# Second-half lower weights by a ScalarE negation and an accumulating transfer in the even layer

## Chip, cores and metric

One core of one Trainium2 chip runs the kernel. The metric is the device time of one execution in microseconds (us); lower is better.

## What is computed

Two layers of a post-norm encoder trunk on 256 tokens of width 2048, in fp32. Both layers are `x = LN(alpha*x + mixer(x))`, then `x = LN(alpha*x + relu(x @ w1)**2 @ w2)`. Only the mixer of the first ("even") layer is touched:

```python
h = x @ w_in
u = h[..., :S5_WIDTH]
q, k, v, gate = jnp.split(h[..., S5_WIDTH:], 4, axis=-1)
...
y = jax.nn.gelu((y_fwd + y_bwd + d_skip.astype(F32) * uf).reshape(bsz, L, S5_WIDTH))
s5_out = (y * jax.nn.sigmoid(y @ w_glu.astype(F32) + b_glu.astype(F32))).astype(x.dtype)
...
ret_out = (o.reshape(bsz, L, RET_WIDTH) * jax.nn.silu(gate.astype(F32))).astype(x.dtype)
return jnp.concatenate([s5_out, ret_out], axis=-1) @ w_out
```

`y_fwd` and `y_bwd` are diagonal state-space scans over the sequence in both directions ("S5"), `o` is retention, a decayed linear attention.

## The kernel before

All weights (356 chunks of 1 MB) pass once through the core in chunks of 512 x 512 numbers, in the order that `weight_order` lists. In this text chunk *n* is the *n*-th of that list, counted from 0: chunks 0 to 39 are `even_w_in`, 40 to 47 `even_w_out`, 48 to 51 `w_glu`, 52 to 59 `even_w_out` again, and then come the two MLPs and the odd layer.

Matmuls run in fp32r, a rounded fp32, so each fp32 number is taken as an upper half (the number rounded to fp32r) plus a lower half (the number minus its upper half), and a product is three matmuls: upper x upper, upper x lower, lower x upper (`mm3`, L186 to L188). `wload` prepares a chunk: a transfer on SP's queue writes it into the tile `wraw` (L169), and then for each of the two halves *b* of the chunk (two of its four 128-row slices each) ScalarE copies it into `whi`, rounding (L178), and VectorE writes `wlo = wraw - whi` (L179).

There are two `wraw` buffers. The transfer of chunk *n* therefore waits until the last reader of chunk *n - 2* is done. In the even layer `whi` and `wlo` have four buffers each, which is two chunks, so half *b* of chunk *n* also waits until TensorE is through with half *b* of chunk *n - 2*. `weights` fetches one chunk ahead. TensorE wants the second half of a chunk in the middle of that chunk's matmuls.

Beside the weights, VectorE and ScalarE work on the S5 mixer and on retention. This work is hung on a table of ticks (one tick is one chunk, each with three phases: `pre`, `mid`, `post`): `s5_plan` starts at tick 7. `s5_in` builds `Fm` on VectorE, turns it on TensorE (L635), multiplies (L645) and turns again (L654); `s5_scan` is a chain of small VectorE operations on `G`; `s5_out` builds `Em` on VectorE, copies `bb` and `G` into `stg` on ScalarE (L696 to L701) and multiplies (L712, L716). Its part `kern` sends a small table `kc` to DRAM (`kd`, L733), `load_m` reads it back in eight transfers (`Mt`, L739), and `load_y` fetches the result (`yg`, L768). `kd`, `Mt`, `yg` and the four `u_dr` stores (L983) are issued by GpSimd (POOL); everything else by SP. `run_phase` places the work of a tick after the two instructions `self.after` that `wload` returned for the chunk. The framework then settles the order on each engine; an engine takes its instructions in that order, and a waiting instruction holds all behind it.

Of the kernel before, what the change touches and what calls it, by code (L numbers as in the profile page):

```python
# [10 lines left out]
F32 = mybir.dt.float32  # L11
# [3 lines left out]
ALU = mybir.AluOpType  # L15
# [36 lines left out]
class Trunk:  # L52
# [54 lines left out]
    def weight_order(self):  # L107
# [6 lines left out]
        for l in r2:  # L114
            if l == 1:
                o += [("odd_w_in", n, kc) for n in (4, 5, 0, 1, 2, 3) for kc in r4]
                o += [("odd_w_out", *x) for x in self.ODD_OUT] + [("odd_w_out", 3, kc) for kc in r4]
            for g in range(NG + 1):
# [22 lines left out]
    AS, AT, AO = 0, 6, 8  # L141

    W1, W2 = 6, 3
    ODD_OUT = [(0, 0), (0, 1), (0, 2), (1, 0), (1, 1), (1, 2), (0, 3), (1, 3), (2, 0), (2, 1), (2, 2), (2, 3)]

    def weights(self, name, *idx):
# [15 lines left out]
    def wload(self, src):  # L162

        nc = self.nc
        raw = self.wp.tile([128, 4, 512], F32, name="wraw", tag="wraw")

        first = self.wnext == 1
        for part in ((slice(0, 2), slice(2, 4)) if first else (slice(0, 4),)):
            self.last = nc.sync.dma_start(raw[:, part], src[:, part]).ins  # L169
        res = []  # L170
        for b in range(2):
            pool = self.wpools[self.wcount % len(self.wpools)]
            self.wcount += 1
            hi = pool.tile([128, 2, 512], F32R, name="whi", tag="whi")
            lo = pool.tile([128, 2, 512], F32R, name="wlo", tag="wlo")
            r = raw[:, 2 * b:2 * b + 2, :]
            for k in ((slice(0, 1), slice(1, 2)) if first else (slice(0, 2),)):
                c = nc.scalar.copy(hi[:, k], r[:, k]).ins  # L178
                d = nc.vector.tensor_tensor(lo[:, k], r[:, k], hi[:, k].bitcast(F32), op=ALU.subtract).ins  # L179
            res += [(hi[:, 0, :], lo[:, 0, :]), (hi[:, 1, :], lo[:, 1, :])]  # L180
        return res, (c, d)

# [996 lines left out]
    def odd_out(self, mix, hp):  # L1179
# [11 lines left out]
        if hp is None:  # L1191
            self.gemm_n(lhs, self.ODD_OUT, 4, src, evac)
            return
# [126 lines left out]
```

## Time and profile before

| what | value |
|---|---|
| median of 3 runs | 2149.88 us (2149.59 to 2151.16) |
| profiled execution: its own time | 2148.78 us |
| profiled execution: span of the trace | 2147.0 us |
| TensorE (PE) busy | 2117.7 us, 99% |
| VectorE (DVE) busy | 1449.6 us, 68% |
| ScalarE (ACT) busy | 1010.9 us, 47% |
| GpSimd (POOL) busy | 57.2 us, 3% |
| mean granted TensorE clock | 0.997 |

The even layer's mixer fills about the first 440 us of the span. Shares over the whole span hide what holds in that part, so it has to be read by stretches. A busy TensorE row includes time in which matmuls overlap in the pipeline: the step from one matmul of 512 columns to the next is about 0.23 us, while the row of one lasts about 0.39 us.

### The profile page before, as it was taken

Reading aid. Unit: us, or ns where it says so; the run is one execution under the profiler, and the core shown is the slowest. Engines: PE = TensorE matmul, PEld = TensorE weight load, DVE = VectorE, ACT = ScalarE, POOL = GpSimd, SP = SyncE. Lnnn points to the kernel's source line nnn. Section 1 sums busy time; section 2 is a strip of 40 time slices with the busy share of each in tenths; the row PEclk is TensorE's granted clock in tenths of the full one; section 3 lists DMA queues with packets and bytes.
Section 4 is the critical chain, followed back from the end, with each engine's and each line's share of the span. In section 5 each row is a group of like instructions: output and inputs, shape, how many; then the busy total and the mean of one; then the engine's idle time right before and its main releaser. Section 6 shows DMA issues by size and latency. Waiting matters only on the chain.

```text
span 2147.0 us, 28354 instructions
## 1 busy us (share of the span) xinstructions
PE 2117.7 (99%) x11218; PEld 1768.9 (82%) x11218; DVE 1449.6 (68%) x2098; ACT 1010.9 (47%) x1387; POOL 57.2 (3%) x102
## 2 busy tenths in 40 slices
PE   9998999999999999999999999999999999999998
PEld 8786777878888888888888888888888888888886
DVE  8999986787655656656566777667555655656556
ACT  4554465564443444434445556465443444434441
POOL 0000232000000000000000000000000000000000
PEclk9999999999999999999999999999999999999999
DMA  8534567565555555555555644555555555555562
GB/s 266 178 119 137 155 193 224 194 227 206 195 188 187 194 189 187 192 194 182 194 196 197 207 150 139 171 193 205 196 185 189 195 188 187 194 191 183 195 231 102
DMA packets 82550, 402.35 MB, mean 187 GB/s; under 512 B 30833, under 2 KB 31089, under 8 KB 35569
## 3 DMA queue, kind: packets, MB, share of 16 engines
q1 hardware_dynamic: 79280, 393.26, 53.9%
q0 software_dynamic: 3136, 7.28, 1.4%
q8 instruction: 88, 1.44, 0.3%
q14 instruction: 46, 0.37, 0.1%
HBM read 395.33 MB, written 5.18 MB: 187 GB/s over the span
## 4 chain that ended last, share of the span: by engine, by line
PE 91%; DVE 7%; issue 0%; DMA 0%; ACT 0%; POOL 0%; SPq 0%; DVEq 0%; POOLq 0%
PE ps L281 22%; PE ps L186 18%; PE ps L188 18%; PE ps L187 18%; PE ps L282 11%; DVE wlo L179 2%; DVE G L64 1%; DVE xt L64 1%; DVE sc L64 1%; PE ps L716 1%; PE ps L635 1%; PE ps L349 0%; DVE Fm L64 0%; DVE Em L64 0%; DMA x<-in_x_dram 0%
## 5 line engine op out<-in xcount | busy, mean ns | idle before, releaser
L179 DVE TENSOR_TENSOR wlo<-wraw,whi 128x1024 fp32r<-128x1024 f32 (+1 forms) x714 | 867.3, 1220 | 619.9 <-ACT whi L178 619.2
L178 ACT CAST whi<-wraw 128x1024 fp32r<-128x1024 f32 (+1 forms) x714 | 746.3, 1050 | 982.7 <-PE ps L188 567.0
L281 PE MATMUL ps<-xt,whi 128*128 128x512 f32 x2048 | 722.3, 397 | 0.0
L282 PE MATMUL ps<-xt,wlo 128*128 128x256 f32 x2048 | 575.0, 281 | 0.0
L281 PEld LDWEIGHTS ps<-xt,whi 128*128 128x128 f32 x2048 | 384.9, 188 | 93.1
L186 PE MATMUL ps<-whi,hh 128*128 128x512 f32 (+1 forms) x1032 | 400.4, 388 | 0.0
L188 PE MATMUL ps<-whi,hl 128*128 128x512 f32 (+1 forms) x1032 | 400.1, 388 | 0.0
L187 PE MATMUL ps<-wlo,hh 128*128 128x512 f32 (+1 forms) x1032 | 399.9, 387 | 0.0
L282 PEld LDWEIGHTS ps<-xt,wlo 128*128 128x128 f32 x2048 | 387.3, 189 | 0.5
L188 PEld LDWEIGHTS ps<-whi,hl 128*128 128x128 f32 x1032 | 193.8, 188 | 40.2
L186 PEld LDWEIGHTS ps<-whi,hh 128*128 128x128 f32 x1032 | 193.8, 188 | 39.8
L187 PEld LDWEIGHTS ps<-wlo,hh 128*128 128x128 f32 x1032 | 193.8, 188 | 39.0
L186 PE MATMUL ps<-whi,xt 128*128 128x512 f32 x512 | 207.1, 405 | 0.2 <-ACT whi L178 0.2
L187 PE MATMUL ps<-wlo,xt 128*128 128x512 f32 x512 | 200.7, 392 | 1.3 <-DVE wlo L179 1.3
L188 PE MATMUL ps<-whi,xt 128*128 128x512 f32 x512 | 201.5, 394 | 0.0
L188 PEld LDWEIGHTS ps<-whi,xt 128*128 128x128 f32 x512 | 96.1, 188 | 21.8 <-issue 1.3
L187 PEld LDWEIGHTS ps<-wlo,xt 128*128 128x128 f32 x512 | 96.4, 188 | 20.5 <-DVE wlo L179 1.7
L186 PEld LDWEIGHTS ps<-whi,xt 128*128 128x128 f32 x512 | 96.1, 188 | 19.9 <-issue 1.8
L64 DVE TENSOR_TENSOR acc<-ps,acc 128x512 f32<-128x512 f32 (+1 forms) x113 | 72.4, 678 | 16.9 <-PE ps L188 16.9
L102 ACT COPY s<-ps 128x256 f32<-128x256 f32 x120 | 42.8, 374 | 25.1 <-PE ps L282 24.9
L92 POOL TENSOR_TENSOR rstd<-rs_ve,mhalf 128x1 f32<-128x1 f32 x8 | 6.9, 857 | 1765.3 <-DVE rs_ve L77 1765.3
L186 PE MATMUL ps<-whi,om 128*128 128x512 f32 x128 | 50.5, 395 | 0.0
(212 smaller groups left out, 1679.7 us busy)
## 6 DMA issues: line engine op xcount, KB each, us to landing
wraw<-in_mlp_w_dram SPq DMA_DIRECT2D x256, 1024.0 KB, 4.9
wraw<-in_even_w_in_dram SPq DMA_DIRECT2D x39, 1024.0 KB, 5.0
wraw<-in_odd_w_in_dram SPq DMA_DIRECT2D x24, 1024.0 KB, 4.9
wraw<-in_even_w_out_dram SPq DMA_DIRECT2D x16, 1024.0 KB, 5.0
wraw<-in_odd_w_out_dram SPq DMA_DIRECT2D x16, 1024.0 KB, 4.8
Mt<-kd POOLq DMA_DIRECT2D x64, 64.0 KB, 3.9
wraw<-in_w_glu_dram SPq DMA_DIRECT2D x4, 1024.0 KB, 4.8
lng<-in_ln_g_dram SPq DMA_DIRECT2D x4, 1024.0 KB, 6.9
```

The lines of the kernel that those rows point to most:

```text
L64: self.nc.vector.tensor_tensor(o, a, b, op=op)
L92: self.nc.gpsimd.tensor_tensor(out, ve, self.mhalf[:, 0:w], op=ALU.pow)
L102: self.nc.scalar.copy(lo[:, i], ps[i][:, 1])
L178: c = nc.scalar.copy(hi[:, k], r[:, k]).ins
L179: d = nc.vector.tensor_tensor(lo[:, k], r[:, k], hi[:, k].bitcast(F32), op=ALU.subtract).ins
L186: nc.tensor.matmul(o, lhsT=ah, rhs=bh, start=first, stop=False)
L187: nc.tensor.matmul(o, lhsT=ah, rhs=bl, start=False, stop=False)
L188: nc.tensor.matmul(o, lhsT=al, rhs=bh, start=False, stop=last)
L281: nc.tensor.matmul(o, lhsT=wh[:, c], rhs=x, start=(k == 0), stop=False)
L282: nc.tensor.matmul(o[:, 0], lhsT=wl[:, c], rhs=x[:, 0], start=False, stop=(k == 4 * nk - 1))
L635: nc.tensor.transpose(ps[:, i * 128:(i + 1) * 128], st["F"][:, r, i, :], self.ident)
L716: nc.tensor.matmul(y[64 * (i % 2):64 * (i % 2) + 64, i // 2 * 128:i // 2 * 128 + 128], lhsT=S[:, r, i, 32:96], rhs=E[:, r, i, :], start=Fa ...
```

## The change

For chunks 6 to 48 (`wnext` counts from 1, so `DMA_LO` is 43 chunks), the second half no longer gets its lower half from VectorE. ScalarE writes `whi` as before, and also writes minus the raw weights, rounded to fp32r, into `wlo`; a transfer issued by GpSimd then adds the raw weights onto `wlo` in place. The first half of these chunks, and all other chunks, are as before. `wload` returns as second member of `self.after` the last VectorE subtraction, which in these chunks is that of the first half.

```diff
+    DMA_LO = range(7, 50)
...
             r = raw[:, 2 * b:2 * b + 2, :]
-            for k in ((slice(0, 1), slice(1, 2)) if first else (slice(0, 2),)):
-                c = nc.scalar.copy(hi[:, k], r[:, k]).ins
-                d = nc.vector.tensor_tensor(lo[:, k], r[:, k], hi[:, k].bitcast(F32), op=ALU.subtract).ins
+            if b == 1 and self.wnext in self.DMA_LO:
+
+                c = nc.scalar.copy(hi, r).ins
+                nc.scalar.mul(lo, r, -1.0)
+                nc.gpsimd.dma_start(lo.bitcast(F32), r, accum_op=ALU.add)
+            else:
+                for k in ((slice(0, 1), slice(1, 2)) if first else (slice(0, 2),)):
+                    c = nc.scalar.copy(hi[:, k], r[:, k]).ins
+                    d = nc.vector.tensor_tensor(lo[:, k], r[:, k], hi[:, k].bitcast(F32), op=ALU.subtract).ins
```

In the changed kernel all lines from here on stand 2 to 8 further down: L178 is L181 or L186, L179 is L187, L186 to L188 are L194 to L196; L182 is the negation and L183 the transfer.

ScalarE, one chunk in the middle of `s5_in` (chunks 22 and 23). Before:

```order
L178 CAST whi<-wraw 128x1024
L649 COPY Vs<-ps 128x256
L636 COPY FT<-ps 128x512 x2
L178 CAST whi<-wraw 128x1024
L658 COPY G<-ps 128x2x128
L178 CAST whi<-wraw 128x1024
```

In the changed kernel:

```order
L181 CAST whi<-wraw 128x1024
L657 COPY Vs<-ps 128x256
L644 COPY FT<-ps 128x512 x2
L186 CAST whi<-wraw 128x1024
L666 COPY G<-ps 128x2x128
L182 ACTIVATE wlo<-wraw 128x1024
L181 CAST whi<-wraw 128x1024
```

The negation is one more ScalarE instruction per chunk; here it stands ahead of the copy of the second half, as in 15 of the 43 chunks; in the other 28 (6 to 14, 25, 30, 31 and 33 to 48) it stands behind it.

GpSimd, two of the eight S5 output groups (`kd`, `Mt`, `yg`). Before:

```order
L733 DMA kd<-kc 128x240
L768 DMA yg<-yd 128x256
L739 DMA Mt<-kd 16x8x128 x8
L733 DMA kd<-kc 128x240
L768 DMA yg<-yd 128x256
L739 DMA Mt<-kd 16x8x128 x8
```

In the changed kernel:

```order
L741 DMA kd<-kc 128x240
L776 DMA yg<-yd 128x256
L183 DMA wlo<-wraw 128x1024
L747 DMA Mt<-kd 16x8x128 x8
L183 DMA wlo<-wraw 128x1024
L741 DMA kd<-kc 128x240
L776 DMA yg<-yd 128x256
L183 DMA wlo<-wraw 128x1024
L747 DMA Mt<-kd 16x8x128 x8
L183 DMA wlo<-wraw 128x1024
```

Every second accumulating transfer of this stretch stands behind the eight `Mt` issues, which wait for `kd` to land.

TensorE, the second half of chunk 8. In the changed kernel:

```order
L194 MATMUL ps<-whi,xt 128x512
L195 MATMUL ps<-wlo,xt 128x512
L196 MATMUL ps<-whi,xt 128x512
L194 MATMUL ps<-whi,xt 128x512 x2
L195 MATMUL ps<-wlo,xt 128x512
L196 MATMUL ps<-whi,xt 128x512
L195 MATMUL ps<-wlo,xt 128x512
```

A matmul with the upper half has been put ahead of the first one with the lower half of that chunk's second part (the row with x2). In the even layer of the kernel before, such a pair stands at two places, the first halves of chunks 8 and 10; in the changed kernel it stands at 16, most of them in second halves of chunks 33 to 46.

## Rows read from the trace of the kernel before

**Rows 1.** The page, parts 1 and 2: whole span, then 40 slices.

```profile
PE 2117.7 (99%) x11218; PEld 1768.9 (82%) x11218; DVE 1449.6 (68%) x2098; ACT 1010.9 (47%) x1387; POOL 57.2 (3%) x102
...
DVE  8999986787655656656566777667555655656556
```

**Rows 2.** Busy time by stretch (us; then PE clock, DMA share, GB/s).

```profile
60.00:200.00 140.00, 135.01 (x903) 106.58 (x904) 134.64 (x276) 75.65 (x127) 2.18 (x3) 1.00 0.44 145
200.00:300.00 100.00, 94.53 (x726) 70.13 (x724) 96.15 (x225) 53.48 (x101) 25.18 (x47) 0.98 0.56 161
300.00:350.00 50.00, 49.75 (x360) 37.68 (x356) 34.61 (x64) 26.73 (x45) 18.64 (x35) 1.00 0.80 235
350.00:440.00 90.00, 90.00 (x437) 74.55 (x438) 64.32 (x78) 45.86 (x59) 1.14 (x2) 1.00 0.56 193
500.00:1150.00 650.00, 650.00 (x3268) 550.98 (x3267) 381.37 (x418) 280.41 (x321) 0.00 (x0) 1.00 0.56 191
```

**Rows 3.** Waits of PE, 60 to 440 us: total us, times, longest.

```profile
PE ps L716 <- ACT stg L699: 2.8, 1, 2.8
PE ps L712 <- DVE Em L64: 2.7, 2, 2.1
PE ps L712 <- DVE Em L82: 2.0, 2, 1.0
PE ps L187 <- DVE wlo L179: 1.3, 1, 1.3
```

**Rows 4.** Timeline of ScalarE at the scan's end.

```profile
195.60 0.82 ACT L699 COPY stg<-G 64x248 f32<-64x248 f32 x2 [8.25 <-DVE G L64]
```

**Rows 5.** Busy time by stretch: the one at the lower clock.

```profile
208.40:211.80 3.40, 3.36 (x28) 2.65 (x29) 3.40 (x8) 1.29 (x5) 0.00 (x0) 0.52 0.00 0
```

**Rows 6.** Groups of instructions by line and form, 60 to 440 us.

```profile
L179 DVE TENSOR_TENSOR wlo<-wraw,whi 128x1024 fp32r<-128x1024 f32 x105 | 127.1, 1220 | 31.5 <-ACT whi L178 31.0
L178 ACT CAST whi<-wraw 128x1024 fp32r<-128x1024 f32 x105 | 109.1, 1051 | 119.8 <-PE ps L188 83.0 <-DMA wraw<-in_even_w_out_dram 16.0 <-PE ps L281 5.2
```

**Rows 7.** DMA issues: count, KB each, median us to landing.

```profile
u_dr<-u POOLq DMA_DIRECT2D x4, 256.0 KB, 2.9
...
wraw<-in_mlp_w_dram SPq DMA_DIRECT2D x256, 1024.0 KB, 4.9
...
xr<-in_x_dram SPq DMA_DIRECT2D x2, 1024.0 KB, 9.3
```

**Rows 8.** The tile wraw, 69.6 to 80 us: chunks 10, 11 and 12.

```profile
DMA to landing us min/median/max: 4.8/5.7/7.6
```

**Rows 9.** Timelines of SP, ACT and PE: chunks 8 and 10.

```profile
69.70 0.43 SPq L169 DMA_DIRECT2D wraw<-in_even_w_in_dram  x1
70.23 0.38 SPq L169 DMA_DIRECT2D wraw<-in_even_w_in_dram  x1
...
59.84 2.00 ACT L178 CAST whi<-wraw 128x1024 fp32r<-128x1024 f32 x2
75.44 2.00 ACT L178 CAST whi<-wraw 128x1024 fp32r<-128x1024 f32 x2 [1.67 <-DMA wraw<-in_even_w_in_dram]
...
65.62 0.39 PE L187 MATMUL ps<-wlo,xt 128*128 128x512 f32 x1
80.80 0.39 PE L187 MATMUL ps<-wlo,xt 128*128 128x512 f32 x1
```

**Rows 10.** Timelines of PE and DVE: first uses in chunks 42, 45, 46.

```profile
340.25 1.23 DVE L179 TENSOR_TENSOR wlo<-wraw,whi 128x1024 fp32r<-128x1024 f32 x1 [1.48 <-ACT whi L178]
351.39 0.39 PE L187 MATMUL ps<-wlo,rr 128*128 128x512 f32 x1
366.48 0.39 PE L187 MATMUL ps<-wlo,rr 128*128 128x512 f32 x1
371.92 0.39 PE L187 MATMUL ps<-wlo,rr 128*128 128x512 f32 x1
```

**Rows 11.** Timelines of POOL and PE: an S5 output group; chunks 12 and 41.

```profile
61.24 0.72 POOL L983 DMA_DIRECT2D u_dr<-u  x1 [20.89 <-DVE u L64]
218.82 0.61 POOL L733 DMA_DIRECT2D kd<-kc  x1 [13.17 <-DVE G L64]
223.17 4.20 POOL L739 DMA_DIRECT2D Mt<-kd  x8 [3.74 <-DMA kd<-kc]
...
93.17 0.39 PE L187 MATMUL ps<-wlo,xt 128*128 128x512 f32 x1
340.93 0.40 PE L187 MATMUL ps<-wlo,rr 128*128 128x512 f32 x1
```

## Prediction

> **What bounds the kernel now.** Read the page first: over the span TensorE is busy 99%, VectorE 68% [rows 1]. By that, relief for VectorE is worth nothing. The line of 40 slices below it says otherwise for the start: VectorE is near full in the first seven slices. So the second view is the busy time by stretch [rows 2]: from 60 to 300 us VectorE is busy 134.6 + 96.2 of 240 us, in the MLP 381 of 650. In the same 240 us TensorE is busy 229.5, and in the MLP all of its time. TensorE sets the end; what can be won is the time for which it waits in the even layer, no more.
>
> Third, its waits there [rows 3]. Four entries of 2.8, 2.7, 2.0 and 1.3 us make 8.8. Three name VectorE. The largest names ScalarE's copy into `stg`, but that copy itself stood 8.25 us for VectorE's scan on `G` [rows 4], so it is VectorE too. After these waits TensorE ran for 3.4 us at a clock of 0.52, its lower level [rows 5]; at the full clock that work takes half, so 1.7 us more is lost. **At most 10.5 us can be won**, 0.5% of the run.
>
> **What the change takes away.** 43 subtractions of 1.22 us [rows 6] leave VectorE, 52 us in all. 27 of them (chunks 8 to 34) lie between 60 and 300 us: 33 us off a stretch in which it is busy for 231 of 240. Its backlog should dissolve, and I count all four waits and the clock as won: **-10.5 us**.
>
> **What it adds.** ScalarE gets 43 negations. No row shows this form; I price it like the copy of the same size, 1.05 us [rows 6], together 45 us. ScalarE has room (53 of 100 us busy at the worst [rows 2]). GpSimd gets 43 issues; the store of 256 KB occupied it for 0.72 us [rows 11], so about 31 us on an engine that is idle for 97%: nothing by themselves. The wait that matters is another: `wlo` of the second half is done when a transfer has landed, and `wraw` is free for the load after the next only then too.
>
> **The price of one accumulating transfer** (512 KB read, 512 KB read and added to, 512 KB written) stands in no row. Below, a plain transfer: between 256 KB in 2.9 us and 1 MB in 4.9 us [rows 7], a third of the way, gives 3.6 us. That counts only the bytes that are moved. If both things it reads count, it is like a load of 1 MB, 4.9 us alone. It is seldom alone, since the DMA engines are busy for half of the time [rows 2]; where two loads were issued 0.5 us apart the median was 5.7 and the longest 7.6 us [rows 8, 9]. Nothing excludes a slower addition; the slowest median of a 1 MB transfer is 9.3 us [rows 7], which I take as the upper end. I take 5.7 us, the nearest row for 1 MB of reading beside another transfer, and 5.7 us for the load beside it.
>
> Here a rule stands against the trace. The rows for 256 KB and 1 MB give 3.6 us for 512 KB. The Trainium skill ("DMA: Bandwidth & Descriptors", section on the anatomy of one DMA) fits a GpSimd transfer as 2.0 us plus the bytes at 436 GB/s; that is an estimate of 3.2 us for 512 KB, and by it the sum would be that of the first rival below. [...]
>
> **Three places where this costs.** The two `wraw` buffers form a ring. One turn takes a load 5.7, two copies 2.0 [rows 9], the negation 1.05, the transfer 5.7: 14.45 us, and must take no longer than two chunks on TensorE.
>
> *Start of the ring.* Chunk 8: the copies end at 59.84 + 2.00 = 61.84 [rows 9], negation to 62.9, landing at 68.6. TensorE took that half at 65.62, after the 1.3 us wait that I count as won, so would want it at 64.3: it waits 4.3. Chunk 10: the load is issued at 69.70, held there by the `U` transfers ahead of it on SP's queue and not by the ring; copies end at 77.4, landing at 84.2; wanted at 80.80 - 1.3 + 4.3 = 83.8: 0.4. Together **+4.7 us**.
>
> *End of the ring.* From chunk 43 the S5 work is over and TensorE takes a chunk in 5.44 us [rows 10], two in 10.88. The ring is 3.57 short per two chunks, so 10.7 us over chunks 43 to 48. There is a lead: in chunk 42 `wlo` was ready at 341.48 and wanted at 351.39 [rows 10], 9.9 us; the new path is longer by 1.05 + 5.7 - 1.23 = 5.5, leaving 4.4. So 10.7 - 4.4 = **+6.3 us**. These are chunks in which VectorE has 26 of 90 us free [rows 2]: there the change relieves nobody.
>
> *Between.* From chunk 12 to 41 a chunk takes (340.93 - 93.17)/29 = 8.54 us [rows 11], two 17.1: the ring fits. But on GpSimd's queue every second transfer from chunk 26 on stands behind `Mt`: this waits until `kd` has landed (4.35 us from issue to issue) and issues for 4.20 us [rows 11]. A transfer that meets it lengthens its turn to 18.65. That is 1.55 over, for one turn in two, and the lead of some 10 us swallows most; where chunks are shorter than the mean it does not. DMA engines are also 80% busy from 300 to 350 [rows 2]. I put **+2 us**, from 0 to 8. SP's queue: the loads now wait for a landing, and `c` and `yd` behind them with it; at 5.7 us the landing comes about when VectorE's late subtraction did in this stretch (the scan held ScalarE and VectorE for 8 us [rows 4]), so nothing.
>
> **Sum:** -10.5 + 4.7 + 6.3 + 2 = **+2.5 us** on the profiled 2148.78, that is 2151.3; the median lies 1.1 higher: **2152.4 us**. A measurement of this kernel can tell about 0.2%, or 4.3 us, from no change.
>
> **Rivals.**
>
> *A cheap transfer (faster).* At 3.6 us with loads at 4.9 the ring turns in 11.55. Chunk 8 lands at 66.5, a wait of 2.2; chunk 10 at 82.1, 0.4. In chunks 43 to 48 the ring is short by 0.34 per chunk, 2.0, under the lead of 6.5: nothing. Between, 15.75 with `Mt` fits too. Sum -10.5 + 2.6 = -7.9: **2142 us**. For it: the small transfers land in 2.9 us. Against: three streams, not two. Chance 0.33.
>
> *A dear transfer (slower): the ring becomes the bound.* The point is 17.1 us per turn, a transfer of 8.3 us with loads at 5.7; up to there it costs at the three places alone. At 7.6 us [rows 8] the turn is 16.35: chunk 8 and 10 give 6.2 + 0.4, the end (16.35 - 10.88)/2 x 6 = 16.4 less a lead of 2.5 is 13.9, between 5 (turns behind `Mt` 3.4 over, half of 16 chunks, less the lead). Sum -10.5 + 6.6 + 13.9 + 5 = +15: **2165 us**. At 9.3 us the turn is 18.05: 0.5 us for each of 29 chunks comes on top, 14, with 8 at the start, 20 at the end and 10 between, **2191 us**. Against it: no transfer of this size took that long in most stretches. For it: an addition in the transfer is unknown, and the order on TensorE has 16 places, not 2, where an upper half is put ahead of a late lower half. Chance 0.18.
>
> *ScalarE becomes late.* The first copy of a chunk now stands at the head of ScalarE until a later load lands, with `G`, `Vs` and `stg` behind it. If that keeps half of the waits, the gain is 5.2, not 10.5: +7.7, **2157.6 us**. For it: TensorE's largest wait already ended on a ScalarE copy. Against: ScalarE is half idle. Chance 0.09.
>
> **How the numbers follow.** My forecast gets 0.40, by itself 2146 to 2158 (transfer between 4.9 and 6.3 us). Faster by over 0.2% is nearly all of the cheap transfer and 0.05 of the forecast: 0.37. Within 0.2%: 0.26 of the forecast and little of the rest, 0.27. Slower: 0.09 of the forecast, the dear transfer, late ScalarE: 0.36. The range goes from a transfer at 2.9 us (chunk 8 lands 0.7 earlier, and 1 us for rows that disagree: 2140) to one at about 8.3 us: 2175. It leaves out the upper half of the dear case and little below.
>
> **What would show it.** In the changed trace: the median from issue to landing of `wlo<-wraw` (5.7 by the forecast, under 4.3 or over 6.5 by the rivals); TensorE's waits on `stg` and `Em` gone; new waits of TensorE for `wlo` at chunks 8, 10 and 45 to 48 and hardly elsewhere; VectorE at 80 to 85% from 60 to 300 us; the low clock gone. If waits for `wlo` are spread over all chunks, the ring binds and I am wrong; if there are none, I overpaid for the transfer; if `stg` and `Em` still hold TensorE, the relief of VectorE was not what they waited for.

## Result and profile after

| what | before | changed |
|---|---|---|
| median of 4 runs | 2150.52 us | 2207.01 us (2204.76 to 2212.54) |
| span of the profiled execution | 2147.0 us | 2204.4 us |
| ratio of the medians, 95% interval | | 1.0265 [1.0252, 1.0277] |

The changed kernel is 56.5 us slower. The forecast was 2152.4 us, and the range ended at 2175.

Busy time by stretch of the changed kernel, in the columns of [rows 2] (PE, PEld, DVE, ACT, POOL, then the PE clock, the DMA share, GB/s):

```profile
60.00:200.00 140.00, 124.20 (x779) 96.71 (x779) 104.80 (x226) 78.92 (x123) 15.06 (x18) 0.96 0.74 190
200.00:300.00 100.00, 91.76 (x690) 69.54 (x689) 86.55 (x223) 56.48 (x107) 30.35 (x50) 0.97 0.82 205
300.00:350.00 50.00, 46.68 (x367) 34.16 (x365) 27.72 (x49) 30.71 (x57) 17.54 (x30) 0.97 0.91 210
350.00:440.00 90.00, 72.40 (x374) 54.72 (x371) 30.90 (x51) 37.06 (x45) 20.29 (x32) 0.96 0.83 219
```

VectorE did get its relief: 104.80 us busy where it was 134.64. TensorE lost more. Two columns say where to look: the DMA engines, busy for 0.44 to 0.80 of the time before, are now busy for 0.74 to 0.91, and the granted clock is at 0.96 to 0.97 in all four stretches. That costs up to 13.7 us, where in [rows 2] it costs up to 2.

TensorE's waits of 60 to 440 us in the changed kernel, to be held against [rows 3] (all the waits of before in this stretch make 10.3 us, these 47.5):

```profile
PE ps L761 <- DVE y L64: 15.8, 5, 6.4
PE ps L195 <- DMA wlo<-wraw: 12.3, 6, 3.6
PE ps L662 <- ACT Vs L657: 5.2, 3, 3.3
PE ps L290 <- DMA wlo<-wraw: 4.3, 2, 4.1
PE ps L643 <- DVE Fm L64: 3.4, 3, 3.0
PE ps L194 <- ACT whi L186: 2.3, 3, 1.2
PE ps L720 <- DVE Em L64: 1.3, 1, 1.3
```

The waits of [rows 3] have shrunk as forecast: `stg` is gone, and `Em` has fallen from 4.7 to 1.7 us (with 0.4 us on L82). In their place stand 16.6 us for the transferred `wlo`, and 15.8 us for `y`, a tile of the S5 output part that no line of the change touches.

DMA issues of 60 to 440 us (count, KB each, median us from issue to landing). Before, the same view had 5.0 for `wraw<-in_even_w_in_dram`, 3.9 for `Mt`, 2.8 for `yd`, 3.8 for `yg`:

```profile
wraw<-in_even_w_in_dram SPq DMA_DIRECT2D x31, 1024.0 KB, 5.9
wlo<-wraw POOLq DMA_DIRECT2D x41, 512.0 KB, 5.8
...
Mt<-kd POOLq DMA_DIRECT2D x64, 64.0 KB, 6.2
...
yd<-yv SPq DMA_DIRECT2D x64, 16.0 KB, 5.0
yg<-yd POOLq DMA_DIRECT2D x8, 128.0 KB, 5.0
```

The new transfer lands in 5.8 us in the median, almost the 5.7 of the forecast. But single ones took from 4.5 to 11.3 us, and 12 of the 43 took more than 7.6. The loads and small transfers of these lines have all become slower beside it.

One turn of a `wraw` buffer in the changed kernel, chunk 12 to chunk 14 (timelines of SP, ACT, POOL, SP: start, us, instruction; the number in brackets is the idle time before it):

```profile
92.71 0.33 SPq L171 DMA_DIRECT2D wraw<-in_even_w_in_dram  x1
99.85 1.05 ACT L186 CAST whi<-wraw 128x1024 fp32r<-128x1024 f32 x1 [2.38 <-DMA wraw<-in_even_w_in_dram]
100.81 1.05 ACT L181 CAST whi<-wraw 128x1024 fp32r<-128x1024 f32 x1
101.76 1.05 ACT L182 ACTIVATE wlo<-wraw 128x1024 fp32r<-128x1024 f32 x1
103.10 0.84 POOL L183 DMA_DIRECT2D wlo<-wraw  x1 [10.45 <-ACT G L666]
107.75 0.33 SPq L171 DMA_DIRECT2D wraw<-in_even_w_in_dram  x1
```

The turn takes 15.04 us: 7.14 until the copy starts, 2.96 for copies and negation, 0.29 of handing over, 4.65 from issue to the next load. The next turn of this buffer takes 16.4 (to 124.19). Of the 43 loads that need a buffer back from a transfer (chunks 8 to 50), 34 are issued within 0.2 us of its landing, and SP waits for these landings 35 times, 249.9 us in all:

```profile
SPq L171 <- DMA wlo<-wraw: 249.9, 35, 11.8
```

SP stood for about as long before: 97.9 us for VectorE's subtraction, and 252.5 us with the entries that name VectorE's other instructions. So the waiting itself is not the loss; the later end of it is. The median turn of a buffer, from load to load, grew from 15.0 to 16.0 us for chunks 10 to 24, and from 17.7 to 20.0 us for chunks 25 to 42.

Nine loads come later still than the landing that frees their buffer. Five of these (chunks 34, 36, 38, 40 and 42, by 1.0 to 6.5 us) stand behind the eight `yd` issues of an S5 output group on SP's queue. Such a group of issues takes 3.6 to 4.7 us before, and 4.5 to 14.9 us in the changed kernel. The longest is the one behind the two `xr` transfers (timelines of SP: before; then in the changed kernel, with SP's wait for `xr`):

```profile
331.21 4.72 SPq L763 DMA_DIRECT2D yd<-yv  x8
```

```profile
355.68 14.93 SPq L771 DMA_DIRECT2D yd<-yv  x8
371.64 3.75 SPq L171 DMA_DIRECT2D wraw<-in_even_w_out_dram  x2
SPq L771 <- DMA xr<-in_x_dram: 10.4, 2, 5.7
```

The first of the two loads at 371.64 is that of chunk 42. Its buffer was free at 365.11, when the transfer of chunk 40 had landed.

How a late load reaches the S5 part is seen at 384 to 397 us (timelines of ACT, DVE, PE of the changed kernel):

```profile
394.47 1.04 ACT L186 CAST whi<-wraw 128x1024 fp32r<-128x1024 f32 x1 [9.76 <-DMA wraw<-in_even_w_out_dram]
395.55 1.22 DVE L187 TENSOR_TENSOR wlo<-wraw,whi 128x1024 fp32r<-128x1024 f32 x1 [5.06 <-ACT whi L186]
396.69 0.42 DVE L64 TENSOR_TENSOR y<-ps,y 128x256 f32<-128x256 f32 x1
397.16 0.69 PE L761 MATMUL ps<-ident,y 128*128 128x128 f32 x2 [5.03 <-DVE y L64]
```

ScalarE's copy of the first half of chunk 44 waits for a load that was issued late: at 387.29, on the landing of chunk 42's transfer, whose own load had stood behind `yd`. VectorE's subtraction waits for the copy. `y` stands behind the subtraction in VectorE's order, and TensorE stands for `y`, which had nothing to do with weights. The wait of 3.3 us for `y` at 337 us has the same chain, behind the load of chunk 38. In the longest one, 6.4 us at 279 us, `y` stands behind VectorE's scan on `G`; why the scan is late there was not followed further.

Last, a thing at the LayerNorm behind the even layer. VectorE's timeline before, and then in the changed kernel:

```profile
443.67 0.15 DVE L77 TENSOR_SCALAR rs_ve<-mv 128x1 f32<-128x1 f32 x1
444.52 1.46 DVE L79 TENSOR_SCALAR acc<-acc,mv,rstd 128x512 f32<-128x512 f32 x3 [0.69 <-POOL rstd L92]
```

```profile
495.81 0.14 DVE L77 TENSOR_SCALAR rs_ve<-mv 128x1 f32<-128x1 f32 x1
497.17 2.36 DVE L187 TENSOR_TENSOR wlo<-wraw,whi 128x1024 fp32r<-128x1024 f32 x2 [1.22 <-ACT whi L186]
499.45 1.91 DVE L79 TENSOR_SCALAR acc<-acc,mv,rstd 128x512 f32<-128x512 f32 x4
```

In the changed kernel two subtractions have come ahead of the normalisation, and one of them waits for its copy. TensorE waits 5.7 us for `acc` there, before 1.4:

```profile
PE ps L357 <- DVE acc L79: 5.7, 1, 5.7
```

The last accumulating transfer had landed at 436.24, so this comes from the order on VectorE and not from a transfer under way. The granted clock fell in that wait too, to 0.50 from 498.95 to 505.78 us.

Where the time was lost can be read from the first use of `wlo` in each chunk; how much later it comes than before is called the delay here: +0.1 us at chunk 7, +5.3 at 8, +10.2 at 9, +22.9 at 24, then +15.1 at 26 (VectorE's waits of 195 to 212 us, won back), +28.8 at 41, +50.1 at 49, +50.6 at 58, +57.6 at 60 behind the LayerNorm.

### The profile page after: what moved, and what is told of

Same layout as the page of the kernel before. It is cut to its first block, busy times and chain, and to the rows that moved or that the text cites. A ratio compares the mean times of both kernels' runs of the same rounds, so it can differ in the third digit from the quotient of the medians.

```text
span 2204.4 us, 28496 instructions
## 1 busy us (share of the span) xinstructions
PE 2132.1 (97%) x11218; PEld 1775.0 (81%) x11218; DVE 1408.1 (64%) x2055; ACT 1042.7 (47%) x1428; POOL 96.1 (4%) x145
## 3 DMA queue, kind: packets, MB, share of 16 engines
q1 hardware_dynamic: 79280, 393.26, 52.9%
## 4 chain that ended last, share of the span: by engine, by line
PE 85%; DMA 8%; DVE 3%; issue 1%; ACT 1%; SPq 1%; POOL 0%; DVEq 0%; ACTq 0%; POOLq 0%
PE ps L289 22%; PE ps L194 16%; PE ps L195 16%; PE ps L196 16%; PE ps L290 11%; DMA wlo<-wraw 3%; DMA wraw<-in_even_w_in_dram 2%; DMA wraw<-in_even_w_out_dram 1%; DVE wlo L187 1%; PE ps L357 1%; DMA wraw<-in_w_glu_dram 1%; DMA yd<-yv 1%; DVE G L64 0%; ACT whi L186 0%; DMA x<-in_x_dram 0%
## 5 line engine op out<-in xcount | busy, mean ns | idle before, releaser
L187 DVE TENSOR_TENSOR wlo<-wraw,whi 128x1024 fp32r<-128x1024 f32 (+1 forms) x671 | 815.2, 1220 | 659.4 <-ACT whi L186 659.1
L186 ACT CAST whi<-wraw 128x1024 fp32r<-128x1024 f32 (+1 forms) x671 | 701.3, 1050 | 974.5 <-PE ps L196 493.9
L194 PE MATMUL ps<-whi,hh 128*128 128x512 f32 (+1 forms) x1032 | 400.5, 388 | 0.0
L196 PE MATMUL ps<-whi,hl 128*128 128x512 f32 (+1 forms) x1032 | 400.1, 388 | 0.0
L196 PEld LDWEIGHTS ps<-whi,hl 128*128 128x128 f32 x1032 | 193.8, 188 | 40.1
L194 PEld LDWEIGHTS ps<-whi,hh 128*128 128x128 f32 x1032 | 193.8, 188 | 39.6
L194 PE MATMUL ps<-whi,xt 128*128 128x512 f32 x512 | 208.9, 410 | 0.5 <-ACT whi L186 0.5
L196 PE MATMUL ps<-whi,xt 128*128 128x512 f32 x512 | 203.1, 397 | 0.0
L196 PEld LDWEIGHTS ps<-whi,xt 128*128 128x128 f32 x512 | 97.4, 190 | 21.3 <-issue 0.2
L194 PEld LDWEIGHTS ps<-whi,xt 128*128 128x128 f32 x512 | 97.3, 191 | 20.9 <-issue 2.0
L182 ACT ACTIVATE wlo<-wraw 128x1024 fp32r<-128x1024 f32 x43 | 45.5, 1057 | 11.7 <-PE ps L195 11.7
```

The costliest lines, as they stand in the source:

```text
L182: nc.scalar.mul(lo, r, -1.0)
L194: nc.tensor.matmul(o, lhsT=ah, rhs=bh, start=first, stop=False)
L196: nc.tensor.matmul(o, lhsT=al, rhs=bh, start=False, stop=last)
```

## Experiments

Four theories, and a fifth from the lines above. **S**: ScalarE is late by its 43 new instructions. **R**: the ring of two `wraw` buffers is too slow, because a buffer is free only when a transfer has landed. **L**: TensorE itself stands for the landing of `wlo`. **C**: the transfers crowd the DMA engines, and loads and small transfers get slower for all. **O**: the order at the LayerNorm. All edits are made on the changed kernel, at L182 and L183, in `DMA_LO`, or in the order of the two halves. They are called n1 (no transfer), n2 (negation and VectorE), n3 (another source), n4 (plain transfer), n5 (crowd alone), n6, n7 and n9 (end, middle and start alone), n8 (GpSimd), n10 (every third chunk), n11 (second half first) and n12 to n14 (few chunks). The changed order on TensorE got no edit of its own. In n1 and n5 an upper half stands ahead of a lower one at two places, as before the change, so what this order does is inside the difference between them and the versions that transfer into `wlo`.

### Without the transfer

```diff
                 nc.scalar.mul(lo, r, -1.0)
-                nc.gpsimd.dma_start(lo.bitcast(F32), r, accum_op=ALU.add)
```

> Edit: the transfer is left out; the negation stays, so the lower halves of these 43 second halves are minus the rounded weights, and the adding of the raw weights is left out. Theory R (ring: the landing of the transfer frees wraw, so the next load but one comes late): wraw is free after the negation, a ring turn is load 5 + copies 1.9 + negation 1.05, about 8.5 us, well below the 10.9 us that TensorE takes for two chunks at its fastest, and VectorE's 52 us are relieved: about 2140 us, 2137 to 2146, with no wait of TensorE on wlo. Theory C (the transfers crowd the DMA engines for everybody): the same, it can't be told apart here. Theory S (43 more ScalarE instructions are what is late): stays above 2185 us.

Measured: 2142.06 us, ratio 0.9957 [0.9942, 0.9972]. So VectorE's relief was worth what the forecast took for it, about 9 to 10 us, and the new ScalarE work does not eat it. This is the floor for every version below.

### Negation, and VectorE as before

```diff
                 nc.scalar.mul(lo, r, -1.0)
-                nc.gpsimd.dma_start(lo.bitcast(F32), r, accum_op=ALU.add)
+                d = nc.vector.tensor_tensor(lo, r, hi.bitcast(F32), op=ALU.subtract).ins
```

> Edit: the negation stays on ScalarE, but the lower half is then written by VectorE's subtraction as in the kernel before; no transfer. It is the kernel before with 43 ScalarE instructions of 1.05 us more. Theory R and theory C: VectorE's late subtraction comes one negation later, nothing else, 2150 to 2158 us. Theory S: above 2185 us.

Measured: 2154.06 us, ratio 1.0009 [0.9999, 1.0018]. Theory S has fallen: 43 negations cost nothing that can be told.

### Another source for the transfer

```diff
-                nc.gpsimd.dma_start(lo.bitcast(F32), r, accum_op=ALU.add)
+                nc.gpsimd.dma_start(lo.bitcast(F32), hi.bitcast(F32), accum_op=ALU.add)
```

> Edit: the accumulating transfer stays, with the same bytes, issue and destination, but adds the upper half whi instead of wraw; the lower halves of these 43 second halves come out as zero, so their product is left out of the result. Nothing reads wraw after ScalarE's negation. Theory R: the ring turn is load 6 + copies 1.9 + negation 1.05, 9 to 10 us, and doesn't bind; wlo itself still lands some 5.5 us later than by VectorE, which costs at chunks 8 and 10 (about 4 to 6 us) and a little at the end, against 8 to 10 us won from VectorE: 2140 to 2156 us; the SP queue's wait on wlo landings (250 us over 35 loads in the changed kernel) is gone. Theory C: the transfers take the same share of the DMA engines, so at least 2/3 of the loss stays: above 2185 us.

Measured: 2187.56 us, ratio 1.0164 [1.0149, 1.0179], just inside what theory C expected. SP's waits for landings of `wlo` are gone, so the ring is out, and 20 us come back; 45 us over n1 stay. Its DMA issues over the whole run, and its longest waits of TensorE:

```profile
wraw<-in_even_w_in_dram SPq DMA_DIRECT2D x39, 1024.0 KB, 6.9
...
wlo<-whi POOLq DMA_DIRECT2D x43, 512.0 KB, 8.8
```

```profile
PE ps L195 <- DMA wlo<-whi: 15.3, 4, 6.9
PE ps L761 <- DVE y L64: 12.6, 5, 3.7
PE ps L290 <- DMA wlo<-whi: 4.0, 2, 3.8
```

With the ring gone the loads come earlier, meet the transfers, and both get slower (8.8 instead of 5.8 us for the transfer; DMA engines 0.97 busy from 300 to 350 us). By these rows the ring had also kept them apart. So what lies between n3 and the change is the ring less what it saved.

### A plain transfer

```diff
-                nc.gpsimd.dma_start(lo.bitcast(F32), r, accum_op=ALU.add)
+                nc.gpsimd.dma_start(lo.bitcast(F32), r)
```

> Edit: the transfer is a plain one, wlo is overwritten by the raw weights instead of adding them, so the subtraction is left out. It still reads wraw, so the ring is as in the change. If the addition is what makes the transfer dear, its median falls from 5.8 to about 3.6 to 4.5 us, the ring turn from 16 to about 14 us, and by theory R the loss falls by more than half: 2150 to 2180 us. If a plain transfer of 512 KB takes as long, the time stays within 10 us of 2207 us. Theory C with bytes read twice being the cost: 2170 to 2195 us.

Measured: 2173.06 us, ratio 1.0104 [1.0087, 1.0121]. 60% of the loss goes with the addition alone, though the median to landing only falls from 5.8 to 4.8 us. The better measure is the time that packets took on GpSimd's queue (q0), as a share of all 16 engines over the span (third number; page, part 3): before, changed, plain.

```profile
q1 hardware_dynamic: 79280, 393.26, 53.9%
q0 software_dynamic: 3136, 7.28, 1.4%
```

```profile
q0 software_dynamic: 9328, 29.83, 6.9%
```

```profile
q0 software_dynamic: 9328, 29.83, 4.1%
```

Worked out per transfer: (6.9% of 2204.4 - 1.4% of 2147.0) / 43 = 2.84 us of all 16 engines for an accumulating one, and 1.37 us for a plain one of the same 512 KB. A load of 1 MB takes about 3.1 us (53.9% of 2147.0 for 393.26 MB, q1 before). So each accumulating transfer occupies the engines nearly like a second load of a whole chunk. The prediction had the bytes right (it took a transfer for "like a load of 1 MB"), but used this for its landing only, and not for what it takes from others.

### The crowd alone

```diff
-                nc.gpsimd.dma_start(lo.bitcast(F32), r, accum_op=ALU.add)
+                for _ in range(2):
+                    nc.gpsimd.dma_start(self.scrap.tile([128, 2, 512], F32, name="scrap", tag="scrap"), hi.bitcast(F32))
```

> Edit: as n1 (negation only, the adding of the raw weights is left out), plus two plain transfers of whi per second half to a DRAM scrap tile that nothing reads, issued by GpSimd where the accumulating one was. n4's plain transfers took 1.4 us of all 16 DMA engines each, the accumulating ones 2.8, so two plain ones stand for one accumulating one. No engine waits for them except through the buffers of whi. n1 was 2142.1, n3 2187.6 us, 45 us more. Theory C (the engines' time taken from loads and small transfers): loads of even_w_in rise from 5.3 to over 6.5 us and most of the 45 us come back, 2170 to 2190 us. Theory L (what counts is that TensorE itself has to wait until wlo has landed, 5 to 9 us after it could have had it): 2142 to 2152 us, though the loads are slower.

Measured: 2166.65 us, ratio 1.0071 [1.0056, 1.0086]: 24.6 us over n1, between the two expectations. The queue's share of the DMA engines, 6.7%, is nearly that of the change. Nothing reads what these transfers write, and they hold others up directly only through the buffers of `whi`. Yet TensorE waits for `y`, 11.4 us instead of 2.8 in n1; `yg` lands in 8.6 us:

```profile
PE ps L762 <- DVE y L64: 11.4, 6, 4.7
PE ps L195 <- ACT whi L187: 3.0, 2, 2.5
```

This supports theory C: the loads take 6.6 us here and the S5 output part's small transfers are slower (`yd` 4.3 us, in n1 2.9). Of the 24 us that lie between the profiles of n1 and n5, 17 arise from chunk 33 to 45, where the last part of that chain runs. How the crowd reaches `y` is followed for one of its six waits only (357.56 us, 1.6 us, behind a weight load issued after `yd`, as above); the two largest, 4.7 and 2.6 us, end on VectorE's own work ahead of `y`. Slow `Mt` transfers alone are not it: n10 below has them at 6.2 us, like the change, and 1.0 us of waits for `y`. The substitute isn't perfect: it writes to DRAM, adds nothing, and keeps `whi` busy longer.

Put in a row, the medians are 2142.1 (no transfer), 2166.7 (crowd), 2187.6 (and TensorE waits for the landing), 2207.0 (and the ring, and the order): **+24.6 for C, +20.9 for L, +19.4 for R and O together**. The 19.3 us for which TensorE waits for landings of `wlo` in n3 agree with the second. O is 7.0 of the last: from chunk 58 to 60 the changed kernel's delay grows from 50.6 to 57.6 us, that of n3 stays at 37.6. The steps are not independent of each other (loads and `Mt` are slower in n3 than in n5), and the kernel before took from 2150.5 to 2152.2 us beside these runs, so the split is rough.

### Place by place

```diff
-    DMA_LO = range(7, 50)
+    DMA_LO = range(44, 50)
```

> Edit: the change for chunks 43 to 48 alone. The prediction's own term for them was +6.3 us with nothing won: 2157 us. A ring turn of 16 us as measured, instead of 14.45, in two chunks of 10.9 us: 5.1 / 2 x 6 = 15.3 less the lead of 4.4, 2162 us. If these chunks cost alone what they cost in the changed kernel (from chunk 41 to 58 its delay grew by 22 us): 2172 us. If the loss needs the lead to have been eaten before: 2150 to 2155 us.

Measured: 2167.1 us, ratio 1.0073 [1.0058, 1.0088]. In the profile 9.0 us arise from chunk 45 to 52 and 4.8 from chunk 58 to 60, the LayerNorm (O: the same two subtractions ahead of it). The first is near the ring at 16 us with its lead of 4.4 (11 us), the second was in no theory.

```diff
-    DMA_LO = range(7, 50)
+    DMA_LO = range(12, 44)
```

> Edit: the change for chunks 11 to 42 alone. By the prediction's terms for the middle (the four VectorE waits and the clock won, 2 us lost): about 2142 us. By the changed kernel's trace, where the delay grew from 11 us at chunk 11 to 29 us at chunk 41 although VectorE was relieved: 2160 to 2175 us, with TensorE waiting for y in the S5 output part and for wlo, and TensorE's low clock in it.

Measured: 2179.72 us, ratio 1.0138 [1.0115, 1.0161], so +28.7, with an interval of 5 us to either side. The delay is 9.9 us at chunk 24, falls to 2.2 at chunk 26, where VectorE's waits were, and then rises to 29.2 by chunk 45. The largest wait is again `y`, 16.1 us. So the stretch from chunk 26 to 45, in which the S5 output part runs, costs some 27 us, three times what the relief wins.

```diff
-    DMA_LO = range(7, 50)
+    DMA_LO = range(7, 12)
```

> Edit: the change for chunks 6 to 10 alone. The prediction's own term for the start was +4.7 us, less up to 10.5 us of VectorE waits that come later: 2145 to 2155 us. If the three places add up (changed kernel +56.5, middle alone +28.7, end alone +16.1 us), the start costs 11.7 us: 2163 us. If what is lost at the start is won back once VectorE has had time, because it stood still for TensorE's waits and not for its own load: about 2151 us, with a delay of about 10 us at chunk 11 that has shrunk below 4 us by chunk 26.

Measured: 2162.46 us, ratio 1.0063 [1.0047, 1.0078]. The three places add up: 12.0 + 28.7 + 16.1 = 56.8 us, against 56.5. Of the start nothing is won back: the delay is 10.4 us at chunk 9 and 10.2 at chunk 26, and the three largest waits of [rows 3] are still there:

```profile
PE ps L195 <- DMA wlo<-wraw: 3.6, 1, 3.6
PE ps L290 <- DMA wlo<-wraw: 3.3, 1, 3.3
PE ps L720 <- DVE Em L64: 3.1, 3, 2.1
PE ps L724 <- ACT stg L707: 2.7, 1, 2.7
PE ps L720 <- DVE Em L82: 2.0, 2, 1.0
```

VectorE was spared five subtractions and had 10 us more while TensorE stood, and TensorE's later waits for it stayed the same. An explanation that fits is that its S5 work is hung on ticks, so that a VectorE that is free early can't work ahead; it was not tested by itself.

### GpSimd in VectorE's place

```diff
-                nc.scalar.mul(lo, r, -1.0)
-                nc.gpsimd.dma_start(lo.bitcast(F32), r, accum_op=ALU.add)
+                nc.gpsimd.tensor_tensor(lo, r, hi.bitcast(F32), op=ALU.subtract)
...
-    DMA_LO = range(7, 50)
+    DMA_LO = range(8, 27)
```

> Edit: no transfer and no negation; in chunks 7 to 25 the second half's lower half is a subtraction on GpSimd instead of VectorE. No row shows this form; bounded by one and three times VectorE's 1.22 us. GpSimd has only 3 other instructions between 60 and 200 us. If VectorE's load was what TensorE waited for (n1 showed 10 us), 19 subtractions fewer should win 5 to 9 us: 2143 to 2148 us. If GpSimd and VectorE slow each other, or GpSimd takes over 4 us: 2150 us or more.

Measured: 2171.38 us, ratio 1.0094 [1.0077, 1.0111], the second case of the expectation. The groups of GpSimd and VectorE from 60 to 300 us in n8 (shapes and count, then busy us and mean ns of one):

```profile
L182 POOL TENSOR_TENSOR wlo<-wraw,whi 128x1024 fp32r<-128x1024 f32 x18 | 49.9, 2774 | 103.5 <-ACT whi L181 92.1 <-PE ps L642 11.4
L186 DVE TENSOR_TENSOR wlo<-wraw,whi 128x1024 fp32r<-128x1024 f32 x36 | 48.2, 1338 | 3.3 <-ACT whi L185 3.3
L64 DVE TENSOR_TENSOR Fm<-Fm,xt 128x512 f32<-128x512 f32 x32 | 26.2, 820 | 0.2
L64 DVE TENSOR_TENSOR xs<-bb 128x64 f32<-128x64 f32 x15 | 16.6, 1107 | 0.0
```

Before, the same three VectorE groups take 1218, 683 and 214 ns. It isn't an even slowing: single instructions are held for long. Of the 15 `xs`, the five that took 2.4 to 4.9 us each ran beside a GpSimd subtraction (the tile's view in n8, duration in ns, least, median and most):

```profile
L64 DVE TENSOR_TENSOR xs<-bb x15: 211/219/4921, 64.7 to 197.3; 128x64 f32<-128x64 f32 x15
```

`Fm` is then late, and TensorE waits 15.4 us for it.

### Fewer transfers, and earlier ones

```diff
-    DMA_LO = range(7, 50)
+    DMA_LO = range(9, 50, 3)
```

> Edit: the change for every third chunk from 8 to 47 alone (14 transfers, in either ring buffer by turns). If the cost is one per transfer (56.5 us over 43, 1.3 us each): 2169 us. If transfers cost by queueing, so that the last ones cost most (crowded DMA engines, ring turns one behind the other with no room to recover), a third of them costs much less than a third: 2146 to 2158 us.

Measured: 2156.93 us, ratio 1.0033 [1.002, 1.0045]. A third of the transfers costs 6.5 us, 12% of the loss. Of these, 5.8 are O (from chunk 58 to 60); up to chunk 58 the delay is 2.0 us. Both losses are what is left after VectorE's relief; with all the 9.2 us of n1 added to either it is 15.7 of 65.7 us, a quarter. So there is no fixed price per transfer: in these runs one costs more where there are more of them, as queueing would have it.

```diff
-        for b in range(2):
+        for b in ((1, 0) if self.wnext in self.DMA_LO else (0, 1)):
...
-            res += [(hi[:, 0, :], lo[:, 0, :]), (hi[:, 1, :], lo[:, 1, :])]
+            res[2 * b:2 * b] = [(hi[:, 0, :], lo[:, 0, :]), (hi[:, 1, :], lo[:, 1, :])]
```

> Edit: the whole change, but ScalarE copies and negates the second half of these 43 chunks ahead of the first half, so the transfer starts one copy (1 us) earlier and a ring turn is that much shorter: 15 us instead of 16. Theory R with L (ring and landing): the ring is 1 us nearer to two chunks' time in each turn, and 20 turns gain 0.5 to 1 us each: 2185 to 2198 us. Theory C alone: within 5 us of 2207 us.

Measured: 2184.1 us, ratio 1.0156 [1.0142, 1.017]. One copy less on the way to the transfer gives back 23 us, with every byte still moved: R and L are a large share of the loss, as n3 and n5 have it. (The edit changes the order on ScalarE as well, which can't be told apart from the shorter way.) `y` falls from 15.8 to 3.1 us and `whi` rises from 2.3 to 10.0. So how long TensorE stands for `y` hangs on what is ahead of it on ScalarE and VectorE, as the lines at 394 us showed, and not on the crowd alone.

```diff
-    DMA_LO = range(7, 50)
+    DMA_LO = range(13, 25, 3)
```

> Edit: the change for chunks 12, 15, 18 and 21 alone, where the trace of before has the second half's lower half ready 7 to 12 us before TensorE takes it, and the DMA engines are busy for about 0.4 of the time. A transfer lands 5.5 us later than VectorE's subtraction, which the lead covers; the chunk between has time to recover. VectorE is relieved of 4.9 us ahead of its waits at 195 to 212 us: 2145 to 2148 us, the first version that would gain. If a transfer costs something even with a lead (as the small transfers of the S5 part do from chunk 26 on), 2150 us or more.

Measured: 2148.92 us, ratio 0.9991 [0.9982, 1.0]. Here the accumulating transfer is undisturbed and lands in 4.5 us, the median of the four. The gain that was expected, 2145 to 2148 us, did not come clear of the noise.

n13 and n14 take the second half first, as n11, with `DMA_LO = range(13, 26)` and with `range(12, 28, 3)`.

> Edit: the change for chunks 12 to 24 alone, second half first as in n11. This leaves out the start, the S5 output stretch with its small transfers, the end and the order at the LayerNorm. Two chunks take 14.7 to 17 us on TensorE there, a turn of the ring about 15 us. If ring and landing alone cost there, a delay of 2 to 6 us at chunk 24, and about 8 us of VectorE's waits won behind it (n7 won 7.7 us from chunk 24 to 26): 2144 to 2149 us. If transfers crowd the loads enough to cost by themselves: 2150 to 2156 us.

> Edit: the change for chunks 11, 14, 17, 20, 23 and 26 alone, second half first. No turn follows a late turn. VectorE is relieved of 7.3 us before or at its waits of 195 to 212 us. n12 with four transfers gave 0.9991 [0.9982, 1.0]. If relief counts in proportion and the transfers cost nothing: 2142 to 2146 us. If what a transfer wins it also costs: 2148 to 2152 us.

Measured: 2148.67 us, ratio 0.9992 [0.9983, 1.0001], and 2149.25 us, ratio 0.9995 [0.9986, 1.0003]. In n13 the delay is 4.1 us at chunk 24 and -2.7 at chunk 26, so 6.8 us of waits are won. Only some 2 were paid on the way, for the delay was 1.9 us already at chunk 12, where the change begins; but the time does not show the rest. In n14 it is 1.6 and -4.9, and back at 2.4 by chunk 30. None of the three can be told from the kernel before, and no version with the whole computation in it gained more than 0.1%.

## Why the prediction was wrong

**The gain, -10.5: right in size.** n1 gives -0.43%, 9.2 us. Behind the transfers some 8 us of it are still won, from chunk 24 to 26.

**One transfer, 5.7 us: right as a median (5.8), too low for the slow ones.** 12 of the 43 took longer than the 7.6 us of the dear-transfer rival (2165 us), and the mean was 6.5. That rival is borne out in part, in the ring; its 9.3 us in general (2191 us) was not needed for a loss of 56 us.

The first rival had a transfer at 3.6 us. An accumulating one never took less than 4.5; a plain one (n4) took 2.8 at least and 4.8 in the median. The fit of the Trainium skill ("DMA: Bandwidth & Descriptors", the anatomy of one DMA) is an estimate of 3.2 us for 512 KB. The fastest plain transfer comes near it, an accumulating one does not.

**The ring, 14.45 us: too short.** For chunks 10 to 24 a turn took 14.0 to 20.1 us, 16.0 in the median; a load took up to 8.1 us and a transfer up to 9.3, where 5.7 was put for each. With that, two chunks of 14.7 us are bound too, and the lead that two terms leaned on is used up before the end comes.

**Start, +4.7: it was 10.2.** The term began at chunk 8. The loss began at chunk 7: in the trace of before its second `wlo` was ready 3.5 us before TensorE took it (53.33 and 56.83), less than the 5.5 us by which the prediction itself made the new way longer. Its transfer met the next load, was issued at 51.70, and TensorE waited 4.1 us for it, until 61.23. The wait at chunk 8, forecast as 4.3 us, came as 3.6.

**Between, +2: the step that failed.** n7 shows +28.7 with the relief in it, so about 36 us of cost. The prediction looked for it where a transfer stands behind `Mt` on GpSimd's queue; but only 3 of 43 transfers were issued more than 1 us after their negation was done (chunks 28, 29 and 41, by 2.5 to 4.2 us). The other way round it happened too: `Mt` issues stood there until a transfer had landed.

```profile
POOL Mt L747 <- DMA wlo<-wraw: 15.1, 4, 7.0
```

What it priced at nothing was SP's queue, with the loads and `yd` behind a landing ("so nothing"), and what a transfer takes from the other transfers. With the DMA engines 0.8 to 0.9 busy, loads went from 5.0 to 5.9 us, `yd` from 2.8 to 5.0 and `Mt` from 3.9 to 6.2. The `yd` issues held SP's queue for up to 14.9 us, the next weight loads stood behind them, and behind a late load stood ScalarE's copy, VectorE's subtraction and `y`. The row that warned was in hand: 0.80 busy from 300 to 350 us before the change [rows 2], to which 2.84 us of every 8.5 were added. How the 36 us divide among these ways is not shown; no run moved `yd` off SP's queue.

**ScalarE becomes late, chance 0.09: it came about.** The third rival had the copy of a chunk at the head of ScalarE until a late load lands, with `Vs` and others behind it. TensorE waits 5.2 us for `Vs` (from 118 to 161 us), before not at all, and the lines at 394 us are the same thing one engine further. The rival priced it at 5.2 us for want of relief; the relief was won, and this came on top.

**End, +6.3: it was 16.1;** in the profile of n6 9.0 by a slower ring and 4.8 by the order at the LayerNorm, which no step looked at.

**The clock: not gone but worse.** The lower level of [rows 5] now comes in all four stretches, with the new waits (as from 62.05 to 65.46 us, at 0.50, after the 4.1 us that TensorE had stood for chunk 7); up to 13.7 us.

Of what the prediction named as a sign that it was wrong, one came in part: waits for the landing of `wlo` outside chunks 8, 10 and 45 to 48. They are at chunks 7, 40 and 42, 6.0 of 16.6 us; the rest is where it was forecast. The larger sign, `y`, was not on its list. In sum, 47.5 - 10.3 = 37.2 us more of waits from 60 to 440 us, 4.3 at the LayerNorm and up to 11.7 of clock (13.7 less 2) make some 53 of the 57.4 us by which the span grew.

## What to carry to other kernels

A transfer that takes over arithmetic is paid three times: by who waits for it, by the buffer it reads from, and by all other transfers, for which its engine time and not its landing time counts. So work out the DMA share of the stretch with it added, and ask which loads stand in one queue behind small transfers that will be slower, and what stands behind such a load on each engine. Relief for a busy engine is won only where TensorE waits for that engine, and what is spared ahead of that place may be lost.

## What was not expected of the hardware

- An accumulating transfer within SBUF took 2.84 us of all 16 DMA engines for 512 KB, a plain one 1.37; to landing, undisturbed, 4.5 us against 2.8 for the fastest plain one.
- A GpSimd subtraction of 128x1024 took 2.77 us, and beside these a VectorE operation of 128x64, of 0.22 us in the median, took up to 4.92 us (before, at most 0.22). The Trainium skill ("GPSIMD Engine Reference", Specifications) says that GpSimd shares its SBUF interfaces with VectorE, with contention for VectorE instructions that have two inputs in SBUF. The trace agrees: the five `xs` that were held all ran beside a GpSimd subtraction.
